# Scale and shift on ScalarE in the opening, two weight operands made there, and LayerNorm, swish, gates and combining issued in separate steps

## The chip, the cores and the metric

The kernel runs on one core of one Trainium2 chip. The metric is the device time of one execution in microseconds (us). Three runs of the kernel before gave 2275.82, 2274.79 and 2270.39 us, with a median of 2274.79.

Five engines work side by side, each with its own queue that it works off in order: TensorE (PE) multiplies matrices, VectorE (DVE) and ScalarE (ACT) do elementwise work and can read PE's results in PSUM, GpSimd (POOL) does elementwise work in SBUF, and SyncE (SP) issues most of the DMAs. An instruction that waits for another engine holds up all that stands behind it in its queue.

## The reference

One layer of a hybrid decoder in float32, for 2048 tokens of a prompt and 8 single tokens (samples), model width 1024:

```python
shift, scale, gate = split(c @ w_c + b_c, 3)
h = x * (1 + scale) + shift
q, k, v, ga, glu, gb, ma, mb = split(h @ w_in + b_in)        # 8704 columns
# A: 12 heads in 3 groups (window, dilation) = (128,1), (512,4), (2048,16), causal, with ALiBi;
#    head j of the three groups is combined, weighted by the groups' softmax denominators
a = (o * silu(ga)) @ w_pa
# B: u = glu; causal depthwise convolution of width 31 -> LayerNorm over 512 channels -> swish
b = (conv * silu(gb)) @ w_pb
y = (sigmoid(ma) * a + sigmoid(mb) * b) @ w_o
x_out = LayerNorm(alpha * x + gate * y)
```

Further outputs are the last k and v rows of each group and the convolution's state.

## The kernel before, in words

**Products.** `h @ w_in` is made in two halves of 1024 tokens (`p` = 0 and 1). Each half is again two blocks of 512 tokens, and the columns of w_in come in pairs of 128-wide tiles. One such pair, over two token blocks and two halves of the inner dimension, is done by a Strassen-like scheme with seven products instead of eight (`quad`, L551). Its left operands (OPS, L34) are sums and differences of the blocks of h, its right operands b11, b21, b22, T1 to T4 are tiles of w_in and differences of them. Every operand is split into a high part, rounded to fp32r by ACT, and a low part, the rest, made by DVE or POOL (L238, L247), and each product is three matmuls: high by high, low by high and high by low (`product`, L489). In the first half a column pair takes 14 products 258 wide (256 tokens and two samples each), in the second half 7 products 512 wide. Products go to PSUM banks X, Z, Y and W; ACT copies part of them out (c1, u2, u3), DVE adds those to the others with the bias and writes a staged tile zst.

**Weights.** `w_make` (L235) makes one right operand: ACT's copy, then the subtraction. `on_dve` (2) gives two of seven of these subtractions to DVE, the others to POOL. In the first half `w_make` also forms T1 to T4 on DVE and stores them to memory; the second half loads them. `MAKE` (L501) and `ahead` (L527) say after which product which operand is made; the second half makes them four products ahead.

**Opening** (L283 to L421). In four blocks b of 256 input columns: 32 matmuls on w_c (`mod_block`), transposes of x into banks X, Y, Z, W (`prep_first`), a copy of the modulation (mrow) and its transposes to scale and shift (`mod_finish`, modT), then `prep_mod`: `part` scales and shifts a transposed block into f (DVE), copies the samples' few columns (ACT), and the seven left operands are formed and split on ACT, DVE and POOL. x is loaded in blocks of 1024 rows by 256, in two buffers. After the opening, operands b11, b21, T2 and T1 of the first pair are made, and the products begin.

**The order of the rest** is set by a count of time kept while the program is written out (`clock`, in us, raised by the estimated length of every product). After every product (in the second half also in the middle of one) `tick` (L474) is called. It takes a step of each lane whose time has come. A lane is a generator, and its `yield 2.6` asks for its next step 2.6 later on that count: `rows_lane` (rows of k and v, and small ends), `at_lane` (attention), `mix_lane` (in the first half samples, then `conv_norm`; in the second `conv_norm`, `combine`, `early_out`) and `smp_lane` (attention of the samples). Convolution steps on DVE fill the rest. `later` puts off a DMA by 2.6.

The parts of it that the change touches:

- `ev_gate` (L705): t = z + bias; ACT's tanh of it into h_; DVE's (h_ + 1) * t, the gate, and its store. All are issued at once.
- `stats` (L817): DVE's mean and variance, three small POOL instructions for rstd and the offset (`rstd_of`, L761), and ACT's Identity that normalizes from PSUM, issued at once.
- `swish` (L828): two ACT instructions and DVE's multiplication, issued at once.
- `conv_norm` (L847): pieces of 256 tokens: load, transpose, `stats` twice, transpose back, `swish` four times, times the gate, store.
- `attention` (L1145): its output Uo has one buffer, which is written by DVE and POOL and stored by DMA.
- `combine` (L1321): 32 items, each a load of three groups' rows; `factors_a` (DVE, then ACT's exponential), `factors_b` (DVE, then ACT scales the first group), `weigh` (four DVE multiply-adds), `turn` (PE transposes, DVE multiplies by the gate, store). One iteration, three steps 1.3 apart: load x and weigh x - 2; factors_a of x - 1; factors_b of x - 1 and turn x - 2.
- `early_out` (L1425) follows `combine` in its lane: it loads and splits w_pa.

A last stage (from L1567) makes a, b, y and the final LayerNorm. It begins with `oc_load`, the loads of what combining and `conv_norm` have stored.

Of the kernel before, what the change touches and what calls it, by code (L numbers as in the profile page):

```python
# [11 lines left out]
OP = mybir.AluOpType  # L12
# [34 lines left out]
def hybrid_layer(ctx: ExitStack, tc: tile.TileContext, I, O):  # L47
# [149 lines left out]
    def w_raw(s, e, x):  # L197
        p, n = stream[s]
        col = col_of(quads[p][n][x])
        if p == 0 and s and e and x:  # L200
            r = raws[s, e, x] = bp.tile([P, 4, P], F32, name="rawb", tag="rawb", bufs=2)
# [33 lines left out]
    def w_make(s, n):  # L235
# [22 lines left out]
        if n == "b11":  # L258
            split(R(0, 0))
        elif n == "b21":  # L260
            split(R(1, 0))
            sub(R(0, 0), R(0, 1), R(0, 0), "T1")
        elif n == "T2":
            t2 = bp.tile([P, 4, P], F32, name="t2", tag="t2")
            sub(t2, R(1, 1), R(0, 0), "T2")
            split(t2)
            sub(R(1, 0), R(1, 0), t2, "T4")
        elif n == "T1":
            split(R(0, 0))
            sub(R(0, 1), R(1, 1), R(0, 1), "T3")  # L270
        elif n == "T3":
            split(R(0, 1))
        elif n == "b22":
            split(R(1, 1))
        else:
            split(R(1, 0))
            for k in [k for k in raws if k[0] == s]:
                raws.pop(k)
# [13 lines left out]

    def x_load(b):
        xs[b] = st.tile([P, 8, 256], F32, name="xs", tag="xs", bufs=2)
        ld(xs[b], I["x_prompt"][0, 0:1024, b * 256:(b + 1) * 256].rearrange("(t p) n -> p t n", p=P))

# [60 lines left out]
    def prep_first(b):  # L357

        pxs = []
        for t in range(2):  # L360
            for e in range(2):
                px = ps("XYZW"[2 * t + e])
                for i in range(4):
                    PE.transpose(px[:, i * P:(i + 1) * P], xs[b][:, 4 * t + i, e * P:(e + 1) * P], ident)
                pxs.append(px)
        pq = ps("U", (P, 2, NB))
        for e in range(2):
            PE.transpose(pq[:, e, :], xsm[:, (2 * b + e) * P:(2 * b + e + 1) * P], ident[:NB, :NB])
        return pxs, pq

    def prep_mod(b, pxs, pq):
# [4 lines left out]
        def part(t, e):  # L376
            kt = 2 * b + e
            f = F[t, e] = st.tile([P, 2 * SUB], F32, name=f"f{t}{e}", tag=f"f{t}{e}")
            v = subs_view(f)
            DVE.tensor_scalar(v[:, :, 0:256], pxs[2 * t + e].rearrange("p (s n) -> p s n", s=2), s1T[:, kt, 0:1], shT[:, kt, 0:1],  # L380
                              op0=OP.mult, op1=OP.add)
            ACT.activation(v[:, :, 256:258], hs[:, e, 4 * t:4 * t + 4].rearrange("p (s n) -> p s n", s=2), AF.Copy)
            return f
# [6 lines left out]
        f["a11"] = part(0, 0)  # L390
        split("a11", DVE)
        f["a12"] = part(0, 1)
        split("a12", POOL)
        part(1, 0)
        f["a22"] = part(1, 1)
        xs.pop(b)
        if b + 2 < 4:
            x_load(b + 2)
        DVE.tensor_tensor(f["s1"], F[1, 0], F[1, 1], op=OP.add)
# [9 lines left out]
    biases()  # L409
    cur = None  # L410
    for b in range(4):
        pm = mod_block(b)
        pre = prep_first(b)
        if b == 0:
            x_load(1)
        if b == 1:
            w_load(0, 0)
            w_load(0, 1)
        mod_finish(b, pm)
        prep_mod(b, *pre)  # L420
    closed(st_cm)  # L421
    bp_cm, bp = opened("bp0", bufs=1)
    wp_cm, wp = opened("wp0", bufs=1)
# [77 lines left out]
    MAKE = {8: (1, "b11"), 9: (1, "b21"), 11: (1, "T2"), 13: (1, "T1"), 0: (0, "T3"), 3: (0, "b22"), 5: (0, "T4")}  # L501
    made = set()

# [201 lines left out]
    def ev_gate(dst, kept, j, col):  # L705
# [3 lines left out]
        def ev(a, u, c, sub):  # L709
            n0, n, sm = span(c, sub)  # L710
            t = stage()
            h_ = stage()
            th = h_[:, :n]
            m = n if sm is None else n + 2
            out_of(t[:, :m], a[:, :m], None if u is None else u[:, :m], b)
            samples_of(kept[:, j, sm], t, sm, n)
            ACT.activation(th, t[:, :n], AF.Tanh, scale=0.5)
            vstt(t[:, :n], th, 1.0, t[:, :n], OP.add, OP.mult)
            gone(h_)
            store(dst[:, c * 512 + n0:c * 512 + n0 + n], t, n)  # L720
        return ev
# [95 lines left out]
    def stats(cv, px, m, out):  # L817
# [7 lines left out]
        POOL.tensor_scalar(sm[:m, 3:4], sm[:m, 0:1], sm[:m, 2:3], -1.0, op0=OP.mult, op1=OP.mult)  # L825
        ACT.activation(out, px[:m], AF.Identity, bias=sm[:m, 3:4], scale=sm[:m, 2:3])

    def swish(pt, yv, i):  # L828
        ACT.activation(yv, pt, AF.Tanh, bias=cgb[:, i, 1:2], scale=cgb[:, i, 0:1])
        ACT.activation(pt, pt, AF.Identity, bias=cgb4[:, i, 1:2], scale=cgb4[:, i, 0:1])  # L830
        vstt(yv, yv, 1.0, pt, OP.add, OP.mult)

    def norm_samples(cv):
        nrm = cv.tile([P, 1054], F32, name="y", tag="y", bufs=2)[:NB, 0:512]
        px = ps("S")
        for i in range(4):
            PE.transpose(px[:NB, i * P:(i + 1) * P], ysS[:, i, :], ident)
        stats(cv, px, NB, nrm)
        yield 6.0
        pt = ps("S", (P, 4, NB))  # L840
        for i in range(4):
            PE.transpose(pt[:, i, :], nrm[:, i * P:(i + 1) * P], ident[:NB, :NB])
        for i in range(4):
            swish(pt[:, i, :], ysS[:, i, :], i)
        yield 1.0

    def conv_norm(cv):  # L847
# [10 lines left out]
        load(pieces[0])  # L858
        yield 5.0
        for x in pieces:  # L860
# [4 lines left out]
            for k in range(2):  # L865
# [3 lines left out]
                clock["pe"] += 0.44  # L869
                stats(cv, px, P, nrm[:, k, :])  # L870
                yield 2.0
            if x + 1 in pieces:
                load(x + 1)
            yield 4.0
            for h in range(2):
# [5 lines left out]
                for i in range(2):  # L881
                    yv = y[:, 2 * h + i, :]
                    swish(pt[:, i, :], yv, 2 * h + i)
                    vtt(yv, yv, sg[:, 2 * h + i, :], OP.mult)
                yield 4.0
            later(lambda y=y, x=x: ld(cg_d[:, :, 256 * x:256 * x + 256].rearrange("i p n -> p i n"), y))
# [258 lines left out]
    def attention(ra, g, j, p, tab, gap, loads, last):  # L1145
# [72 lines left out]
        def s_pv(i):  # L1218
# [4 lines left out]
            for n, (b, prev, s) in enumerate(segs(bts[i])):  # L1223
# [4 lines left out]
                clock["pe"] += 0.22 if prev else 0.11  # L1228
            Uo = ra.tile([P, 4, 130], F32, name="Uo", tag="Uo")
            vcopy(Uo[:, :nb, :P], U[:, :nb, :])  # L1230
# [90 lines left out]
    def combine(cv):  # L1321
# [52 lines left out]
        n = len(work)  # L1374
        for x in range(n + 2):

# [114 lines left out]
    queued = set()  # L1491
    for n in ("b11", "b21", "T2", "T1"):
        make(0, n)
    s = 0
    for p in range(2):
# [44 lines left out]
        if p == 0:  # L1540
# [262 lines left out]
```

## Time and profile before

| what | value |
|---|---|
| median of 3 runs | 2274.79 us |
| the profiled execution | 2272.58 us |
| its span, first to last instruction | 2270.7 us |
| granted TensorE clock, mean over the span | 0.981 |
| instructions | 36385 |
| moved by DMA | 392.08 MB, 173 GB/s |

The page of the profile lists each engine's busy time, the span in 40 slices, the DMA queues, the chain of work that ended last, and the costliest groups of instructions with what ended the idle time before them. Views of the trace show the same by line, by wait, by stretch of time (windows) or in order of time. In a timeline's row stand the start in us, the duration, the engine, the line, the operation, the tiles (written<-read) and the shapes; square brackets hold the idle time of the engine just before it and what ended that. In a row of waits stand the us in total, the number of times and the longest. A line can be that of a helper: L76 and L80 are the helpers for DVE's two-input operations.

### The profile page before, as it was taken

How to read it: one execution, taken by the hardware profiler on the slowest of the kernel's cores; microseconds unless marked ns; L12 is line 12 of the kernel's file. 1: busy time of each engine (PE TensorE's matmuls, PEld its weight loads, DVE VectorE, ACT ScalarE, POOL GpSimd, SP SyncE). 2: the span in 40 equal slices, each digit the busy share in tenths (PEclk: the TensorE clock that was granted, in tenths of full speed). 3: DMA queues.
4: the chain of work that ended last, by engine and by line, in shares of the span. 5: the costliest groups of instructions: out<-in, count | busy, mean ns of one | idle time of the engine just before them, and what ended most of it. 6: DMA issues, size and time to landing. Idle time of an engine off the chain costs nothing.

```text
span 2270.7 us, 36385 instructions
## 1 busy us (share of the span) xinstructions
PE 2124.6 (94%) x13185; PEld 1866.6 (82%) x13185; DVE 1375.4 (61%) x2205; ACT 909.4 (40%) x2056; POOL 833.6 (37%) x866
## 2 busy tenths in 40 slices
PE   6799999999997899989999999999988888999998
PEld 3699999999997768968888888888776667888886
DVE  4667776777676633445777777644556635554556
ACT  2424444444444435644444443456454442111110
POOL 1445454444543333453333333333212235322332
PEclk9899999999999999999999999999999999999999
DMA  8255554456667665445555555568878657334220
GB/s 254 87 171 185 151 180 147 152 163 193 200 201 248 189 195 178 153 111 156 161 178 166 176 148 179 185 191 261 252 237 235 214 176 252 113 121 130 94 95 30
DMA packets 403981, 392.08 MB, mean 173 GB/s; under 512 B 26521, under 2 KB 331213, under 8 KB 402769
## 3 DMA queue, kind: packets, MB, share of 16 engines
q1 hardware_dynamic: 336213, 342.63, 48.8%
q10 hardware_dynamic: 67588, 47.13, 6.5%
q8 instruction: 104, 1.70, 0.3%
q14 instruction: 76, 0.62, 0.1%
HBM read 245.91 MB, written 144.29 MB: 172 GB/s over the span
## 4 chain that ended last, share of the span: by engine, by line
PE 46%; DVE 6%; issue 5%; ACT 4%; DMA 3%; POOL 3%; ACTq 0%; SPq 0%; POOLq 0%; DVEq 0%
PE ps_W L494 8%; PE ps_X L494 8%; PE ps_Z L494 8%; PE py L1743 7%; PE pab L1687 5%; PE ps_Y L494 4%; PE ps_S L1187 3%; PE ps_U L979 1%; POOL bop L247 1%; PE ps_U L1227 1%; DVE yL L76 1%; ACT bop L238 1%; PE ps_S L1212 1%; DVE zst L80 1%; DMA orow<-Uo 1%
## 5 line engine op out<-in xcount | busy, mean ns | idle before, releaser
L247 POOL TENSOR_TENSOR bop<-raw,bop 128x512 fp32r<-128x512 f32 x273 | 397.9, 1459 | 643.2 <-ACT bop L238 584.6
L494 PE MATMUL ps_W<-As,bop 128*128 128x258 f32 (+1 forms) x2448 | 438.8, 328 | 20.5 <-DVE zst L80 19.4
L494 PEld LDWEIGHTS ps_W<-As,bop 128*128 128x128 f32 x2448 | 361.5, 191 | 62.8 <-DVE zst L80 23.6
L80 DVE SCALAR_TENSOR_TENSOR y<-u,cwT,y 128x1024 f32<-128x1024 f32 x240 | 361.1, 1505 | 1.6
L238 ACT ACTIVATE bop<-raw 128x512 fp32r<-128x512 f32 x409 | 251.5, 624 | 79.6 <-DVE raw L76 27.7
L494 PE MATMUL ps_X<-Aa,bop 128*128 128x258 f32 (+1 forms) x1224 | 220.9, 329 | 22.3 <-ACT bop L238 14.0
L494 PE MATMUL ps_Z<-As,bop 128*128 128x258 f32 (+1 forms) x1224 | 224.5, 330 | 7.0 <-ACT u L575 5.7
L494 PE MATMUL ps_X<-As,bop 128*128 128x258 f32 (+1 forms) x1224 | 220.5, 326 | 2.8 <-POOL As L1112 2.2
L494 PE MATMUL ps_Y<-Aa,bop 128*128 128x258 f32 (+1 forms) x1224 | 221.3, 329 | 0.0
L494 PEld LDWEIGHTS ps_X<-Aa,bop 128*128 128x128 f32 x1224 | 183.2, 194 | 43.7 <-ACT bop L238 14.3
L494 PE MATMUL ps_Z<-Aa,bop 128*128 128x258 f32 (+1 forms) x1224 | 217.1, 326 | 1.3 <-ACT smg L605 1.3
L247 DVE TENSOR_TENSOR bop<-raw,bop 128x512 fp32r<-128x512 f32 x136 | 100.6, 739 | 182.1 <-ACT bop L238 178.2
L494 PEld LDWEIGHTS ps_Z<-As,bop 128*128 128x128 f32 x1224 | 180.9, 192 | 27.3 <-ACT u L575 6.3
L494 PEld LDWEIGHTS ps_X<-As,bop 128*128 128x128 f32 x1224 | 179.6, 191 | 22.1 <-POOL As L1112 3.0
L494 PEld LDWEIGHTS ps_Z<-Aa,bop 128*128 128x128 f32 x1224 | 181.0, 191 | 20.1 <-ACT smg L605 1.5
L494 PEld LDWEIGHTS ps_Y<-Aa,bop 128*128 128x128 f32 x1224 | 181.9, 193 | 18.2 <-issue 1.8
L1204 ACT ACTIVATE X<-X,mz 128x128 f32<-128x128 f32 (+1 forms) x192 | 87.0, 454 | 167.8 <-DVE mz L84 160.5
L80 DVE SCALAR_TENSOR_TENSOR zst<-ps_W,bT,c 128x258 f32<-128x258 f32 (+1 forms) x102 | 58.4, 573 | 92.7 <-ACT c L585 90.6
L1640 ACT ACTIVATE xr<-xr,lnm 128x1024 f32<-128x1024 f32 (+1 forms) x16 | 19.9, 1244 | 183.8 <-POOL lnm L1639 183.8
L1687 PE MATMUL pab<-oH,wc0H 128*128 128x256 f32 (+1 forms) x256 | 73.5, 287 | 18.5 <-DVE ev L80 16.1
L1187 PE MATMUL ps_S<-ak,aq 128*128 128x256 f32 (+1 forms) x256 | 90.3, 484 | 0.0
L80 DVE SCALAR_TENSOR_TENSOR zst<-ps_Y,bT,c 128x258 f32<-128x258 f32 (+1 forms) x90 | 51.4, 571 | 56.2 <-PE ps_Y L494 36.5
(309 smaller groups left out, 3743.0 us busy)
## 6 DMA issues: line engine op xcount, KB each, us to landing
raw<-w_in SPq DMA_DIRECT2D x205, 256.0 KB
raw<-tw_d SPq DMA_DIRECT2D x136, 256.0 KB
tw_d<-raw SPq DMA_DIRECT2D x102, 256.0 KB
tw_d<-t SPq DMA_DIRECT2D x34, 256.0 KB
rawb<-w_in SPq DMA_DIRECT2D x33, 256.0 KB
wc<-w_c SPq DMA_DIRECT2D x16, 512.0 KB
aq<-zq SPq DMA_DIRECT2D x16, 512.0 KB
xr<-x_prompt SPq DMA_DIRECT2D x16, 512.0 KB
```

Source lines behind the costliest of these rows:

```text
L76: DVE.tensor_tensor(out, a, b, op=op)
L80: DVE.scalar_tensor_tensor(out, a, s, b, op0=op0, op1=op1)
L238: ACT.activation(t[:, 0], r, AF.Copy)
L247: eng.tensor_tensor(t[:, 1], r, f32(t[:, 0]), op=OP.subtract)
L494: PE.matmul(acc[:, :n], w[:, i, b, :], a[:, b, off:off + n], start=start and b == 0 and x == 0, stop=b == 3 and x == 2, skip_group_check=True)
L979: PE.matmul(po, PZ[:n, g, x, :], t[:n, g, :], start=x == 0 and g == 0, stop=x == NB - 1 and g == 2)
L1187: PE.matmul(S[:, s:s + w, :], q_of(b), k_of(b, w), start=True, stop=True)
L1204: ACT.activation(X[:, s:s + w, :], X[:, s:s + w, :], AF.Exp, bias=mz[:, n, 0:1], accum_out=mz[:, n, 1:2])
L1212: PE.transpose(pt[:, s, :], X[:, s, :], ident)
L1227: PE.matmul(U[:, n, :], Y[:, s, :], v_of(b), start=not prev, stop=True)
L1687: PE.matmul(p[:, :n], a, b[:, kt, :n], start=i == 0, stop=i == 11)
L1743: PE.matmul(py[h], a[:, d, c0:c0 + P], w[:, h * 512:(h + 1) * 512], start=f, stop=l)
```

## The change

- **Opening.** `part`'s scale and shift is an ACT Identity with scale and bias instead of a DVE tensor_scalar, and the samples' columns are copied by POOL instead of ACT. The order of the four parts is a11, a21, a22, a12. x is loaded in half blocks of 512 rows, with three buffers, each half issued when a buffer is free. Operands b11 and b21 of the first pair are made in block 3, ahead of its `mod_finish`; for that, their pool is opened before the opening, and two tiles (rawb, t2) move to another pool.
- **Gates, LayerNorm, swish.** The gate's last multiplication and store are a step of rows_lane 1.4 later. `stats` returns its normalizing activation, and `conv_norm` issues it 2.6 later. The swish's multiplication is issued 2.6 after its activations. The first load of `conv_norm` has 9.0 instead of 5.0 ahead of its use.
- **Combining.** One iteration is now: load x and factors_b of x - 2; factors_a of x - 1; turn x - 3 and weigh x - 2. There is one iteration more.
- **Attention.** Uo has two buffers.
- **Second half.** `on_dve` is 0: all subtractions of the right operands are POOL's.

```diff
+    def x_load(b, ts=(0, 1)):
+        for t in ts:
+            xs[b, t] = st.tile([P, 4, 256], F32, name="xs", tag="xs", bufs=3)
...
-            DVE.tensor_scalar(v[:, :, 0:256], pxs[2 * t + e].rearrange("p (s n) -> p s n", s=2), s1T[:, kt, 0:1], shT[:, kt, 0:1],
-                              op0=OP.mult, op1=OP.add)
-            ACT.activation(v[:, :, 256:258], hs[:, e, 4 * t:4 * t + 4].rearrange("p (s n) -> p s n", s=2), AF.Copy)
+            ACT.activation(v[:, :, 0:256], pxs[2 * t + e].rearrange("p (s n) -> p s n", s=2), AF.Identity, scale=s1T[:, kt, 0:1],
+                           bias=shT[:, kt, 0:1])
+            POOL.tensor_copy(v[:, :, 256:258], hs[:, e, 4 * t:4 * t + 4].rearrange("p (s n) -> p s n", s=2))
...
-        xs.pop(b)
+        if b + 1 < 4:
+            x_load(b + 1, (1,))
         if b + 2 < 4:
-            x_load(b + 2)
+            x_load(b + 2, (0,))
...
+        if b == 3:
+            w_make(0, "b11")
+            w_make(0, "b21")
         mod_finish(b, pm)
         prep_mod(b, *pre)
...
-            vstt(t[:, :n], th, 1.0, t[:, :n], OP.add, OP.mult)
-            gone(h_)
-            store(dst[:, c * 512 + n0:c * 512 + n0 + n], t, n)
+            def end(at):
+                while clock["pe"] < at:
+                    yield 0.3
+                vstt(t[:, :n], th, 1.0, t[:, :n], OP.add, OP.mult)
+                gone(h_)
+                store(dst[:, c * 512 + n0:c * 512 + n0 + n], t, n)
+            rows_lane.add(end(clock["pe"] + 1.4))
...
-        ACT.activation(out, px[:m], AF.Identity, bias=sm[:m, 3:4], scale=sm[:m, 2:3])
+        return lambda: ACT.activation(out, px[:m], AF.Identity, bias=sm[:m, 3:4], scale=sm[:m, 2:3])
...
-                stats(cv, px, P, nrm[:, k, :])
-                yield 2.0
+                apply = stats(cv, px, P, nrm[:, k, :])
+                yield 2.6
+                apply()
...
+                yield 2.6
+                for i in range(2):
+                    yv = y[:, 2 * h + i, :]
+                    swish_end(pt[:, i, :], yv)
                     vtt(yv, yv, sg[:, 2 * h + i, :], OP.mult)
-                yield 4.0
+                yield 1.3
...
-            Uo = ra.tile([P, 4, 130], F32, name="Uo", tag="Uo")
+            Uo = ra.tile([P, 4, 130], F32, name="Uo", tag="Uo", bufs=2)
...
-        for x in range(n + 2):
+        for x in range(n + 3):
...
             if 0 <= x - 2 < n:
-                weigh(x - 2)
+                factors_b(x - 2)
             yield 1.3
             if 0 <= x - 1 < n:
                 factors_a(x - 1)
             yield 1.3
-            if 0 <= x - 1 < n:
-                factors_b(x - 1)
+            if 0 <= x - 3 < n:
+                turn(x - 3)
             if 0 <= x - 2 < n:
-                turn(x - 2)
+                weigh(x - 2)
             yield 1.3
...
+            on_dve[0] = 0
```

More of the change, by code (lines that the diff above doesn't have):

```diff
@@ L200, in w_raw @@
         if p == 0 and s and e and x:
-            r = raws[s, e, x] = bp.tile([P, 4, P], F32, name="rawb", tag="rawb", bufs=2)
+            r = raws[s, e, x] = wp.tile([P, 4, P], F32, name="rawb", tag="rawb", bufs=2)
         else:
@@ L263, in w_make @@
         elif n == "T2":
-            t2 = bp.tile([P, 4, P], F32, name="t2", tag="t2")
+            t2 = wp.tile([P, 4, P], F32, name="t2", tag="t2")
             sub(t2, R(1, 1), R(0, 0), "T2")
@@ L291, in wc_load @@
         ld(wcs[b, h, k], I["w_c"][k * 512:(k + 1) * 512, h * D + b * 256:h * D + (b + 1) * 256].rearrange("(k p) n -> p k n", p=P))
-    def x_load(b):
-        xs[b] = st.tile([P, 8, 256], F32, name="xs", tag="xs", bufs=2)
-        ld(xs[b], I["x_prompt"][0, 0:1024, b * 256:(b + 1) * 256].rearrange("(t p) n -> p t n", p=P))
+    def x_load(b, ts=(0, 1)):
+        for t in ts:
+            xs[b, t] = st.tile([P, 4, 256], F32, name="xs", tag="xs", bufs=3)
+            ld(xs[b, t], I["x_prompt"][0, 512 * t:512 * t + 512, b * 256:(b + 1) * 256].rearrange("(t p) n -> p t n", p=P))
     HK = ((0, 0), (0, 1), (1, 0), (1, 1))
@@ L363, in prep_first @@
                 for i in range(4):
-                    PE.transpose(px[:, i * P:(i + 1) * P], xs[b][:, 4 * t + i, e * P:(e + 1) * P], ident)
+                    PE.transpose(px[:, i * P:(i + 1) * P], xs[b, t][:, i, e * P:(e + 1) * P], ident)
                 pxs.append(px)
@@ L391, in prep_mod @@
         split("a11", DVE)
+        part(1, 0)
+        f["a22"] = part(1, 1)
         f["a12"] = part(0, 1)
         split("a12", POOL)
-        part(1, 0)
-        f["a22"] = part(1, 1)
-        xs.pop(b)
+        if b + 1 < 4:
+            x_load(b + 1, (1,))
         if b + 2 < 4:
-            x_load(b + 2)
+            x_load(b + 2, (0,))
         DVE.tensor_tensor(f["s1"], F[1, 0], F[1, 1], op=OP.add)
@@ L409, in hybrid_layer @@
     biases()
-    cur = None
+    bp_cm, bp = opened("bp0", bufs=1)
     for b in range(4):
@@ L414, in hybrid_layer @@
         if b == 0:
-            x_load(1)
+            x_load(1, (0,))
         if b == 1:
@@ L421, in hybrid_layer @@
     closed(st_cm)
-    bp_cm, bp = opened("bp0", bufs=1)
     wp_cm, wp = opened("wp0", bufs=1)
@@ L501, in hybrid_layer @@
     MAKE = {8: (1, "b11"), 9: (1, "b21"), 11: (1, "T2"), 13: (1, "T1"), 0: (0, "T3"), 3: (0, "b22"), 5: (0, "T4")}
-    made = set()
+    made = {(0, "b11"), (0, "b21")}
     def make(s, n):
@@ L830, in swish, with swish_end @@
         ACT.activation(pt, pt, AF.Identity, bias=cgb4[:, i, 1:2], scale=cgb4[:, i, 0:1])
+    def swish_end(pt, yv):
         vstt(yv, yv, 1.0, pt, OP.add, OP.mult)
@@ L837, in norm_samples @@
             PE.transpose(px[:NB, i * P:(i + 1) * P], ysS[:, i, :], ident)
-        stats(cv, px, NB, nrm)
-        yield 6.0
+        apply = stats(cv, px, NB, nrm)
+        yield 4.0
+        apply()
+        yield 4.0
         pt = ps("S", (P, 4, NB))
@@ L844, in norm_samples @@
             swish(pt[:, i, :], ysS[:, i, :], i)
+        yield 2.0
+        for i in range(4):
+            swish_end(pt[:, i, :], ysS[:, i, :])
         yield 1.0
@@ L858, in conv_norm @@
         load(pieces[0])
-        yield 5.0
+        yield 9.0
         for x in pieces:
@@ L869, in conv_norm @@
                 clock["pe"] += 0.44
-                stats(cv, px, P, nrm[:, k, :])
-                yield 2.0
+                apply = stats(cv, px, P, nrm[:, k, :])
+                yield 2.6
+                apply()
             if x + 1 in pieces:
                 load(x + 1)
-            yield 4.0
+            yield 2.6
             for h in range(2):
@@ L883, in conv_norm @@
                     swish(pt[:, i, :], yv, 2 * h + i)
+                yield 2.6
+                for i in range(2):
+                    yv = y[:, 2 * h + i, :]
+                    swish_end(pt[:, i, :], yv)
                     vtt(yv, yv, sg[:, 2 * h + i, :], OP.mult)
-                yield 4.0
+                yield 1.3
             later(lambda y=y, x=x: ld(cg_d[:, :, 256 * x:256 * x + 256].rearrange("i p n -> p i n"), y))
@@ L1491, in hybrid_layer @@
     queued = set()
-    for n in ("b11", "b21", "T2", "T1"):
+    for n in ("T2", "T1"):
         make(0, n)
```

## The prediction

> **What bounds the kernel now.** I read the page's busy table first, then the view of windows, stage by stage, and then the engines' own timelines where TensorE (PE) stands still.
>
> ```profile
> span 2270.7 us, 36385 instructions
> PE 2124.6 (94%) x13185; PEld 1866.6 (82%) x13185; DVE 1375.4 (61%) x2205; ACT 909.4 (40%) x2056; POOL 833.6 (37%) x866
> ```
>
> PE is busy for 94% of the span, so at most 2270.7 - 2124.6 = 146 us of standing still can be won, beside what a lowered clock costs; the matmuls themselves stay as they are. The windows say where those 146 us lie. Their columns: stretch, its length, then busy us (instructions) of PE, PEld, DVE, ACT and POOL, the granted clock, the DMA share and GB/s.
>
> ```profile
> 0.00:84.00 84.00, 48.20 (x239) 25.42 (x240) 49.39 (x74) 21.04 (x47) 18.39 (x18) 0.85 0.57 172
> 84.00:655.00 571.00, 567.36 (x4581) 559.12 (x4581) 393.70 (x550) 248.72 (x614) 279.13 (x321) 1.00 0.55 170
> 655.00:820.00 165.00, 134.46 (x993) 127.67 (x992) 104.24 (x202) 76.22 (x175) 58.96 (x108) 0.94 0.71 216
> 955.00:1012.00 57.00, 46.10 (x216) 36.67 (x215) 29.85 (x33) 30.83 (x62) 35.27 (x29) 0.94 0.32 94
> 1012.00:1520.00 508.00, 507.35 (x2420) 418.02 (x2419) 342.42 (x374) 221.39 (x485) 168.27 (x146) 1.00 0.56 169
> 1610.00:1725.00 115.00, 101.94 (x485) 83.79 (x483) 68.37 (x199) 55.17 (x162) 22.78 (x26) 0.96 0.80 245
> 1725.00:1826.00 101.00, 86.04 (x364) 65.17 (x365) 69.20 (x209) 46.18 (x107) 25.11 (x20) 0.98 0.71 222
> ```
>
> The long stretches of products, 84 to 655 and 1012 to 1520, have 3.6 and 0.7 us of PE idle in them: whatever the change does to evictions, Uo or splits there is hidden. The idle is in the opening (35.8 us), in the stretch with gates, LayerNorm and swish of the first half (30.5), at the turn between the halves (10.9), and in the combining (13.1 + 15.0). The change has a part in each, so I cost it stage by stage. In each the question is which instruction, waiting at the head of an in-order queue, holds back the work behind it.
>
> **The opening.** Rows of DVE, ACT, POOL and PE from their timelines; the last two are prices from elsewhere.
>
> ```profile
> 53.71 0.20 DVE L352 TENSOR_TENSOR modT<-ps_S,mbias 128x36 f32<-128x36 f32 x1 [0.50 <-PE ps_S L350]
> 67.95 0.20 DVE L352 TENSOR_TENSOR modT<-ps_S,mbias 128x36 f32<-128x36 f32 x1 [0.50 <-PE ps_S L350]
> 70.66 0.81 DVE L380 TENSOR_SCALAR f<-ps_Y,modT 128x512 f32<-128x512 f32 x1
> 79.74 1.35 DVE L387 TENSOR_TENSOR Aa<-f,Aa 128x516 fp32r<-128x516 f32 x1 [0.43 <-ACT Aa L386]
> 82.24 1.75 DVE L76 TENSOR_TENSOR raw<-raw 128x512 f32<-128x512 f32 x1 [1.15 <-POOL bop L247]
> 84.03 0.69 DVE L76 TENSOR_TENSOR t<-raw 128x512 f32<-128x512 f32 x1
> 84.76 0.63 ACT L238 ACTIVATE bop<-t 128x512 fp32r<-128x512 f32 x1 [4.01 <-DVE t L76]
> 85.47 1.28 POOL L247 TENSOR_TENSOR bop<-t,bop 128x512 fp32r<-128x512 f32 x1 [2.02 <-ACT bop L238]
> 80.28 0.80 PE L494 MATMUL ps_X<-Aa,bop 128*128 128x258 f32 x2 [12.37 <-ACT bop L238]
> 86.34 1.94 PE L494 MATMUL ps_X<-As,bop 128*128 128x258 f32 x12
> 768.82 0.78 ACT L826 ACTIVATE y<-ps_S,lnm 128x512 f32<-128x512 f32 x1 [3.38 <-POOL lnm L825]
> 762.07 0.18 POOL L611 COPY smg<-zst 128x2 f32<-128x2 f32 x1 [6.06 <-DVE zst L80]
> ```
>
> A block of the opening lasts 67.95 - 53.71 = 14.2 us, and DVE is its chain: the next block's mrow copy stands behind all of this block's DVE work. The change takes four scale-and-shifts of 0.81 (3.2 us) off DVE and gives them to ACT, where this operation on this shape does not occur; the nearest row is the LayerNorm's Identity from PSUM at 0.78, so about the same, on an engine that is idle most of the block. The small copies go to POOL at 0.18 each. DVE now waits for ACT before its first sum, so I let 2.0 of the 3.2 come through (bounds 0 and 3.2). That holds for two blocks. Ahead of block 3's mrow the change puts a subtraction that waits for POOL (1.75 for itself, and some 0.6 of waiting), so that block gains nothing: 2.0 - 2.4 = -0.4. The last modT comes 3.6 us earlier.
>
> Now the end. Today PE stands 12.37 us for operand b11, because its ACT copy is behind all of block 3. With b11 and b21 made beforehand the first two products run as soon as a11 and a12 are there. The third product needs T2, which still stands behind block 3 on DVE: today DVE ends block 3 at 79.74 + 1.35, 13.1 after modT, and with the 2.0 off at 11.1; then come 0.69, 0.63 and 1.28 (subtraction, ACT, POOL). It starts some 12.4 us after modT, and its third matmul waits until 13.7. Today it starts 86.34 - 67.95 = 18.4 after. I count from the later one, 18.4 - 13.7 = 4.7 won, not 12.37: T2 is late next. Opening: 3.6 + 4.7 = **-8** (bounds -4, if DVE keeps its pace, and -12.4, all of today's wait). The x loads go in halves, with three buffers of half the size; the second half of block 2 is now issued behind the w_in loads on SP, and PE's matmuls on w_c for that block hide its landing; were it late, PE's transposes and DVE's next block would be late by as much.
>
> **Gates, LayerNorm, swish (first half).** A row of the list of ACT's waits, then PE's timeline, and one row of DVE.
>
> ```profile
> ACT y L826 <- POOL lnm L825: 46.8, 16, 6.8
> 697.24 1.09 PE L868 MATMUL ps_S<-ident,u 128*128 128x128 f32 x4 [5.80 <-DMA u<-ysp_d]
> 770.17 2.00 PE L494 MATMUL ps_X<-Aa,bop 128*128 128x258 f32 x12 [2.97 <-ACT smg L605]
> 801.93 2.82 PE L494 MATMUL ps_Z<-As,bop 128*128 128x258 f32 x12 [4.60 <-ACT u L575]
> 667.30 1.60 PE L494 MATMUL ps_Y<-Aa,bop 128*128 128x258 f32 x12
> 658.28 0.43 DVE L80 SCALAR_TENSOR_TENSOR zst<-zst 128x256 f32<-128x256 f32 x1 [0.48 <-ACT zst L717]
> ```
>
> The normalizing activation is issued as soon as its statistics are, and ACT stands 46.8 / 16 = 2.9 us in the mean until POOL has the rstd. Behind it in ACT's queue are the copies that empty PE's banks: that is PE's 2.97 and 4.60. Issued 2.6 later (two ticks, two products of about 1.5), it finds its operand ready, or waits under 1 us. DVE's finishing multiply waits 0.48 for each gate's tanh, and the swish's the same way; behind these are the evictions of bank W. Moved behind other work, both go. The load of u had 5.0 and now has 9.0 to land, so of its 5.80 some 1.5 stay. New waits: PSUM tile S is held longer, and POOL's rstd can stand behind a split. Of 30.5 us I leave 10: **-20** (bounds -10 and -27). Standing still also slows the matmuls after it: 2.82 instead of 1.60. At a granted clock of 0.94 that is 6% of 134.46 = 8 us, of which I take **-5** back (bounds 0 and -8). The same steps in the second half meet no idle and bring nothing.
>
> The Trainium skill ("TensorE: Matmul & The Clock Gate", section on HAM oscillation) has it that the clock drops only behind idle gaps of over about 3.4 us. By that, only three of these gaps (5.80, 4.60 and one in the combining) count and the clock terms would shrink to about half, the sum to some 2230; the trace is less strict, with 2.00 for 1.60 behind a gap of 2.97.
>
> **Splits to POOL, and the turn.** From page part 5, and PE's timeline:
>
> ```profile
> L247 POOL TENSOR_TENSOR bop<-raw,bop 128x512 fp32r<-128x512 f32 x273 | 397.9, 1459 | 643.2 <-ACT bop L238 584.6
> L247 DVE TENSOR_TENSOR bop<-raw,bop 128x512 fp32r<-128x512 f32 x136 | 100.6, 739 | 182.1 <-ACT bop L238 178.2
> 990.59 0.73 PE L494 MATMUL ps_X<-As,bop 128*128 128x512 f32 x2 [1.70 <-POOL As L1112]
> ```
>
> Two in seven splits are DVE's, so 68 of the second half's 238 move to POOL: DVE sheds 68 x 0.74 = 50 us and the waits ahead of them (178.2 / 136 = 1.3 each), POOL gains 68 x 1.46 = 99. One product of the second half is 507 us in 2420 matmuls, 2.5 us a dozen, so POOL keeps up. Only at the turn, where PE already waits for POOL's As, does it bite: one or two splits in the way, **+2** (0 to +4).
>
> **Combining.** PE, then DVE and POOL beside it, then the earlier worst case, then DVE's waits within 1725 to 1826.
>
> ```profile
> 1764.95 0.69 PE L1365 MATMUL ps_S<-ident,y 128*128 128x128 f32 x2 [3.04 <-issue]
> 1762.11 3.01 DVE L80 SCALAR_TENSOR_TENSOR y<-y,csf 128x128 f32<-128x128 f32 x4 [1.04 <-ACT y L1351]
> 1756.17 1.18 DVE L80 SCALAR_TENSOR_TENSOR u<-u,csf 128x128 f32<-128x128 f32 x4
> 1761.86 1.26 POOL L247 TENSOR_TENSOR bop<-raw,bop 128x512 fp32r<-128x512 f32 x1 [3.37 <-ACT bop L238]
> 1674.93 0.74 PE L1365 MATMUL ps_S<-ident,u 128*128 128x128 f32 x2 [5.76 <-DVE u L80]
> 1673.40 0.69 DVE L88 COPY Uo<-ps_U 128x512 f32<-128x512 f32 x1 [6.80 <-DMA orow<-Uo]
> DVE bop L247 <- ACT bop L238: 13.8, 8, 2.1
> DVE csf L76 <- ACT csf L1341: 8.3, 13, 1.6
> ```
>
> PE's transposes stand until DVE has weighed their rows. Weigh and turn were two ticks apart and become three (some 1.5 us more); DVE's waits of 13.8 and 8.3 go, with the splits moved and the exponentials a tick older; the second Uo buffer takes the 6.80. DVE's 69.2 + 27 of waits in 101 us becomes about 80, below PE's 86. Of 28.1 us I leave 9: **-19** (bounds -9 and -25), and of the clock's 6 us (0.04 x 102 + 0.02 x 86) I take **-4**. Loads now wait on SP for the turn four items back, with the fetches of weights queued behind them, five operands ahead of use; a store of that turn's result waited there a tick later already, so I cost it at nothing.
>
> **Handing over.** Combining runs one item more, about 5 us, and the early output weights and the last stage's loads follow it. From the chain and PE's timeline:
>
> ```profile
> 1855.45 6.59 DMA ocr<-cg_d
> 1864.27 0.39 PE L1687 MATMUL pab<-oH,wc0H 128*128 128x256 f32 x1 [2.29 <-ACT oH L1587]
> ```
>
> That load already arrives last, so its delay is PE's: **+5** (0 to +6).
>
> **Sum.** -8 - 20 - 5 + 2 - 19 - 4 + 5 = -49. The profiled execution took 2272.58 us (1.9 beyond its span) and becomes 2223.6; the median of 2274.79 lies 2.2 higher, so 2226. A measurement of this kernel tells about 0.3% (7 us) from no change.
>
> **Rivals.** (1) *The waits move on instead of going.* POOL's rstd comes 2.9 us late today and is asked for 3 us later; behind a longer POOL queue ACT waits anew, and DVE, near PE's pace in combining, keeps turns late. Half of every gain: -4 - 10 - 2.5 - 9.5 - 2 + 7 = -21, so 2254. For it: four stages, all with thin margins. Against: the worst single waits (12.37, 5.80, 5.76, 4.60) each have a clear remedy here.
>
> (2) *POOL's extra splits block DVE.* Beside two POOL splits DVE's four multiplies took 3.01 instead of 1.18, 0.9 for each split. 68 more put up to 68 x 1.46 = 99 us in DVE's way; if each reached PE through a late eviction, the time is 2226 + 99 = 2325, slower than before. It decides from 49 / 68 = 0.72 us of PE time a split. Against it: DVE is busy 342 of 508 us from 1012 to 1520, and 342 + 99 - 50 fits with 117 to spare.
> The Trainium skill ("SBUF — State Buffer", section "Who interferes with whom") says that a VectorE instruction with two SBUF inputs and a GpSimd one that reads SBUF share a port pair, and the later one blocks entirely; by that rule alone this rival stands, and the 3.01 beside 1.18 agrees.
>
> (3) *No net change*: the handover takes more, or memory now shared between opening and products makes b11 wait after all, and the other stages bring little: 0 - 5 + 4 - 9 + 6 = -4, so 2271.
>
> **Chances.** Forecast 0.70, (1) 0.20, (2) 0.05, (3) 0.05. The range reaches down to the sum with all gains near their bounds (4, 7, 6 and for the clock 4 us more: 2205), and up to rival (1), 2254. Faster by over 0.3%: 0.70 + 0.20 = 0.90; within: 0.05; slower: 0.05.
>
> **What would show it.** First product of the opening near 66, third near 78; no ACT wait for lnm above 1 us and PE idle of about 10 us in the gates' stretch; turn's waits under 10 us together; the start of the last stage waiting 5 us longer for ocr. I am wrong if the long product stretches show PE idle for evictions or bop, or if the clock stays at 0.94 to 0.96 without gaps.

## The result, and the profile after

The new kernel takes 2204.66 us, the median of four runs (2202.19 to 2208.26), against 2272.59 (2268.56 to 2275.82) for the kernel before: a ratio of 0.9703, with a 95% interval of 0.968 to 0.9726. That is 68 us less, where 49 were forecast; the median lies at the very edge of the range, 0.3 us below it. The profiled execution took 2208.26 us, and its span is 64.3 us shorter than the one before. The head of the new page:

```profile
span 2206.4 us, 36413 instructions
PE 2109.8 (96%) x13185; PEld 1864.7 (85%) x13185; DVE 1333.1 (60%) x2121; ACT 918.3 (42%) x2056; POOL 930.2 (42%) x950
```

PE is busy for 14.8 us less with the same number of matmuls, and stands still for 97 us instead of 146: so about 50 us are waits that are gone, and 15 us are matmuls that run faster or overlap better. Where that lies is read from windows cut at nearly the same work in both traces (opening, gates' stretch, combining; the counts of matmuls differ by 4 at most). Before, then after; the columns are those of the prediction:

```profile
0.00:86.30 86.30, 50.50 (x253) 27.72 (x254) 51.13 (x77) 22.47 (x50) 19.23 (x19) 0.84 0.57 173
644.00:820.00 176.00, 145.46 (x1084) 138.48 (x1084) 110.73 (x216) 81.78 (x188) 64.62 (x116) 0.94 0.68 210
1607.00:1857.00 250.00, 220.50 (x982) 174.88 (x981) 148.15 (x420) 118.09 (x295) 61.89 (x54) 0.97 0.73 229
```

```profile
0.00:78.50 78.50, 48.85 (x254) 28.02 (x254) 39.47 (x61) 31.61 (x50) 22.92 (x35) 0.89 0.62 191
634.00:787.00 153.00, 135.45 (x1080) 130.75 (x1078) 112.92 (x210) 78.82 (x181) 66.78 (x104) 0.99 0.77 239
1578.80:1794.00 215.20, 210.08 (x985) 173.14 (x983) 145.26 (x404) 115.62 (x294) 85.09 (x72) 0.98 0.85 265
```

The gates' stretch is 23 us shorter: idle 30.5 becomes 17.5, and PE's busy time falls by 10.0 for nearly the same matmuls, with the granted clock at 0.99 instead of 0.94. (By the finer measure below the whole first half wins 20.2, so the stretch won 20 to 23.) Combining is 34.8 us shorter: idle 29.5 becomes 5.1, busy falls by 10.4.

For the experiments a finer measure is wanted. Every run has the same products in the same order, so the start of one product in the trace of before, less its start in another trace, is what that run has won up to there. The marks are the third product of the opening, the first product 512 wide (the start of the second half), the second half's products 100, 165 (ahead of combining) and 237 (its end); the differences between them belong to the stages. In us, with the positive sign for earlier:

| kernel | opening | first half | turn | to product 165 | combining | span |
|---|---|---|---|---|---|---|
| new | 7.9 | 20.2 | -4.0 | 3.3 | 36.1 | 64.3 |
| new, profiled again (e9) | 7.8 | 20.2 | -3.6 | 3.3 | 39.0 | 66.7 |
| e1: opening alone | 7.9 | -1.2 | -0.1 | 0.1 | 1.7 | 7.9 |
| e2: combining's old order | 7.0 | 19.6 | -1.5 | 3.3 | 16.5 | 45.1 |
| e3: splits on DVE too | 8.0 | 19.7 | 0.1 | 2.9 | 25.6 | 55.6 |
| e4: one Uo buffer | 7.1 | 15.7 | -3.6 | 3.3 | 32.7 | 55.4 |
| e5: norm at once | 8.1 | 11.2 | -1.9 | 1.1 | 40.6 | 57.4 |
| e6: gates at once | 7.4 | 23.8 | -3.6 | 2.1 | 37.5 | 66.5 |
| e7: load 5.0 ahead | 7.0 | 14.4 | -1.8 | 2.7 | 37.6 | 59.4 |
| e8: three iterations more | 6.3 | 20.8 | -1.9 | 3.1 | 36.6 | 50.1 |
| e10: T2 in block 3 | 11.9 | 19.2 | -3.8 | 3.3 | 36.6 | 66.8 |
| e11: switch after the turn | 7.1 | 21.3 | 1.5 | 3.3 | 38.4 | 70.0 |
| e12: e10 and e11 | 11.8 | 21.3 | 1.6 | 3.3 | 38.8 | 76.6 |

The eight runs whose code of combining is the new one won between 36.1 and 40.6 us there, two runs of one kernel 36.1 and 39.0. So one trace places a gain in combining to within some 4 us. At the turn, nine runs with the new kernel's code there fall into two groups: -3.6 to -4.0 in five, -1.5 to -1.9 in four (e2, e5, e7, e8). So a figure of one trace can be off by over 2 us there.

Now the places. In the opening, PE and then DVE and ACT of the new kernel:

```profile
64.50 0.59 PE L351 MATMUL ps_S<-ident,mrow 9*128 9x9 f32 x4 [5.71 <-DVE mrow L348]
66.18 2.95 PE L498 MATMUL ps_X<-Aa,bop 128*128 128x258 f32 x12 [1.10 <-ACT f L381]
78.47 3.07 PE L498 MATMUL ps_X<-As,bop 128*128 128x258 f32 x12 [6.67 <-ACT c L568]
```

```profile
65.12 0.19 DVE L353 TENSOR_TENSOR modT<-ps_S,mbias 128x36 f32<-128x36 f32 x1 [0.68 <-PE ps_S L351]
76.28 0.68 DVE L76 TENSOR_TENSOR t<-raw 128x512 f32<-128x512 f32 x1
```

```profile
77.00 0.63 ACT L238 ACTIVATE bop<-t 128x512 fp32r<-128x512 f32 x1 [2.01 <-DVE t L76]
77.53 0.61 ACT L238 ACTIVATE bop<-raw 128x512 fp32r<-128x512 f32 x1
78.05 0.37 ACT L568 ACTIVATE c<-ps_X 128x258 f32<-128x258 f32 x1
```

The first product starts at 66.18 (forecast: near 66), the third at 78.47 (near 78). The third waits 6.67 us, and what ends the wait is not T2 itself: the product writes bank X, and the copy that empties X stands on ACT behind T2's copy, which waits for DVE's t. The head of a queue holds back what is behind it, here once more.

At the turn, PE and POOL:

```profile
963.56 1.22 PE L498 MATMUL ps_X<-As,bop 128*128 128x512 f32 x2 [3.38 <-POOL As L1133]
964.58 5.11 PE L498 MATMUL ps_Z<-Aa,bop 128*128 128x512 f32 x12
```

```profile
958.42 3.42 POOL L247 TENSOR_TENSOR bop<-raw,bop 128x512 fp32r<-128x512 f32 x2
961.80 1.71 POOL L1133 TENSOR_TENSOR As<-Fs,As 128x512 fp32r<-128x512 f32 x1
```

Two splits stand ahead of As in POOL's queue, as forecast; the wait of 1.70 became 3.38, and the product behind it takes 5.11 us instead of 2.95 (the kernel before at 991.16).

For combining, PE's waits from 1530 to 1830, before and after:

```profile
PE ps_S L1365 <- issue: 10.7, 6, 3.0
PE ps_S L1365 <- DVE u L80: 9.0, 4, 5.8
```

```profile
PE ps_S L1386 <- issue: 2.2, 1, 2.2
```

and those of DVE from 1570 to 1830 before. After, DVE makes no split here, and the same waits are 1.5 us for csf and 2.6 for Uo:

```profile
DVE bop L247 <- ACT bop L238: 31.4, 16, 3.4
DVE csf L76 <- ACT csf L1341: 16.4, 22, 1.6
DVE Uo L88 <- DMA orow<-Uo: 16.0, 5, 6.8
```

### The profile page after: what moved, and what is told of

Its sections match the earlier page's. It is cut to its first block, busy times and chain, and to the rows that moved or that the text cites. A ratio compares the mean times of both kernels' runs of the same rounds, so it can differ in the third digit from the quotient of the medians.

```text
span 2206.4 us, 36413 instructions
## 1 busy us (share of the span) xinstructions
PE 2109.8 (96%) x13185; PEld 1864.7 (85%) x13185; DVE 1333.1 (60%) x2121; ACT 918.3 (42%) x2056; POOL 930.2 (42%) x950
## 4 chain that ended last, share of the span: by engine, by line
PE 53%; DVE 4%; DMA 2%; issue 1%; POOL 1%; ACT 1%; ACTq 0%; SPq 0%; POOLq 0%; DVEq 0%
PE ps_Z L498 9%; PE ps_W L498 9%; PE ps_X L498 9%; PE py L1765 8%; PE pab L1709 5%; PE ps_Y L498 4%; PE ps_S L1208 3%; PE ps_U L1248 1%; PE ps_S L1233 1%; DVE yL L76 1%; PE ps_S L653 1%; DVE xr L80 1%; PE ps_U L1246 1%; DVE st L1648 0%; DMA u<-orow 0%
## 5 line engine op out<-in xcount | busy, mean ns | idle before, releaser
L247 POOL TENSOR_TENSOR bop<-raw,bop 128x512 fp32r<-128x512 f32 x341 | 485.8, 1430 | 568.2 <-ACT bop L238 441.3
L247 DVE TENSOR_TENSOR bop<-raw,bop 128x512 fp32r<-128x512 f32 x68 | 51.9, 763 | 94.4 <-ACT bop L238 90.9
L80 DVE SCALAR_TENSOR_TENSOR X<-ps_S,tabh 128x512 f32<-128x512 f32 (+1 forms) x80 | 52.5, 656 | 83.0 <-PE ps_S L1208 76.0
L1662 ACT ACTIVATE xr<-xr,lnm 128x1024 f32<-128x1024 f32 (+1 forms) x16 | 19.9, 1244 | 183.7 <-POOL lnm L1661 171.2
```

The costliest lines, as they stand in the source:

```text
L80: DVE.scalar_tensor_tensor(out, a, s, b, op0=op0, op1=op1)
L247: eng.tensor_tensor(t[:, 1], r, f32(t[:, 0]), op=OP.subtract)
```

## The experiments

The theory: PE stood still because an instruction that waited at the head of an in-order queue (DVE's for a split, an exponential or a store; ACT's for rstd) held back the eviction or the weighing that PE needed; the change removes those waits one by one, each worth its own part. The main rivals: the waits move on and share one gain; POOL's splits block DVE; the handover's step.

**The opening alone (e1).** The kernel before with the opening's part of the diff only.

> The kernel before with the opening's part of the change alone (and the splits moved to POOL in the second half and the new order in combining both left as the new kernel has them is NOT the case here: gates, LayerNorm, swish, Uo are as before; combining and on_dve are as in the new kernel). Theory (each stage keeps what its own waits lose): products of the long stretch start 7 us earlier, the gates' stretch keeps its 30 us of idle, combining gains 20 to 35 us: 2205 + 21 to 25 for the gates' stretch and 3 to 7 for Uo, so 2229 to 2237. Rival (the waits move on, the stages share one gain): removing the gates' steps costs under 10 us, 2205 to 2215.

This text describes another kernel, one with the new combining in it, and its numbers are not for the one that ran, so nothing was forecast for it. By the stages of the traces the opening alone gives its own 8 us, 2265, but that is worked out after the fact. Measured: 2264.92 us, ratio 0.9971 (0.996 to 0.9982), 8.2 us under the 2273.09 of before. The 7.9 us that stand in the table at the third product are still there at the end. So the gain in the opening isn't eaten by later stages.

**Combining's old order (e2).**

```diff
-        for x in range(n + 3):
+        for x in range(n + 2):
...
-                factors_b(x - 2)
+                weigh(x - 2)
...
-            if 0 <= x - 3 < n:
-                turn(x - 3)
+            if 0 <= x - 1 < n:
+                factors_b(x - 1)
             if 0 <= x - 2 < n:
-                weigh(x - 2)
+                turn(x - 2)
```

> The new kernel with combining's old order (weigh x-2; factors_a of x-1; factors_b of x-1 and turn of x-2), all else new. Theory (the order takes the waits for ACT's exponential and for weigh off the heads of the queues): combining loses 15 to 30 of the 35.5 us that it won, 2220 to 2235, with DVE waiting 8 us or more for csf and PE waiting 15 us or more at the turn's transposes. Rival (splits moved to POOL and the second Uo buffer did it by themselves): within 6 us of the new kernel.

2228.06 us, ratio 0.9809 (0.9795 to 0.9822): 23 us over the new kernel. PE's and DVE's waits in combining:

```profile
PE ps_S L1386 <- issue: 10.2, 6, 3.0
PE ps_S L1386 <- DVE u L80: 4.1, 1, 4.1
```

```profile
DVE csf L76 <- ACT csf L1362: 25.9, 25, 2.3
```

The waits at the turn's transposes and those for the exponential are back together. The order is worth some 21 us of combining (16.5 against 36 to 41). How much of that is the later turn and how much the older exponential was not separated.

**Two of seven splits on DVE (e3)**: the line `on_dve[0] = 0` is left out.

> The new kernel with two of seven splits on DVE in the second half, as before. Theory (splits at the head of DVE's queue wait for ACT's copy): the turn gets back 3 us, combining loses 5 to 15, so slower than the new kernel by 2 to 12 us, 2207 to 2217. Rival of the prediction (POOL's extra splits block DVE): faster than the new kernel by 5 us or more. Second rival (with the new order nothing in combining waits for DVE): 2202, faster by the turn's 3 alone.

2216.64 us, ratio 0.9761 (0.9748 to 0.9774): 12 us over the new kernel, the upper end of what the theory gave. The table has 4 us given back at the turn and 10 to 13 lost in combining, where DVE waits again:

```profile
DVE bop L247 <- ACT bop L238: 31.7, 16, 4.3
```

The rival of the prediction had the sign the other way: moving these splits to POOL is worth 12 us net, and the turn is the only place where this trace shows a cost of it.

**One Uo buffer (e4)**: without `bufs=2`.

> The new kernel with one Uo buffer. Theory (a copy into Uo that waits for the store holds DVE's queue): DVE's waits on that store come back, 7 to 13 us in combining, of which PE sees 3 to 7: 2208 to 2212. Rival (hidden behind the deeper order of combining): within 2 us of the new kernel.

2216.36 us, ratio 0.9756 (0.9743 to 0.9769): 12 us over the new kernel, more than either theory gave. DVE's waits on the store are back in combining (20.6 us from 1570 to 1830, where 7 to 13 were expected), and combining loses 3 to 6 us. Another 4.5 are lost in the first half's products, 3.6 of them at one place, which I had counted as covered. PE there, a window around it, and the same place in the kernel before, PE and DVE:

```profile
370.05 2.95 PE L498 MATMUL ps_W<-As,bop 128*128 128x258 f32 x12 [2.08 <-DVE zst L80]
372.80 1.92 PE L498 MATMUL ps_Z<-As,bop 128*128 128x258 f32 x12
```

```profile
369.00:374.00 5.00, 3.95 (x20) 3.95 (x21) 3.55 (x6) 0.35 (x1) 3.00 (x4) 0.66 0.24 79
```

```profile
375.70 1.70 PE L494 MATMUL ps_W<-As,bop 128*128 128x258 f32 x12 [1.98 <-DVE zst L80]
373.63 0.42 DVE L88 COPY Uo<-ps_U 128x256 f32<-128x256 f32 x1 [4.36 <-DMA orow<-Uo]
```

On DVE of e4, a copy into Uo starts 2.1 us ahead of that product, after 4.46 us of idle time, with the eviction of W behind it in the queue. Its row names a product as what ended the wait; the row of the kernel before, for the same copy, names the store of the tile before. In e4 the wait of 2.08 us is followed by products at a granted clock of 0.66 that take 2.95 and 1.92 us instead of 1.60. In the kernel before, a wait of 1.98 us was followed by one of 1.70. So of these 3.6 us the change won about 2 here, the wait; the slow products are e4's own (the last section says what decides on them).

**The norm's activation at once (e5)**: `stats` issues it and returns an empty function.

> The new kernel with LayerNorm's normalizing activation issued at once behind its statistics, as before; all else new. Theory (at the head of ACT's queue it waits 3 us for POOL's rstd, and the copies that empty PE's banks stand behind it): ACT waits 35 to 47 us for lnm again, and of the 21 us that the gates' stretch won, 8 to 15 go: 2213 to 2220. Rival (the waits had moved on to POOL, so the late step brings little): within 4 us of the new kernel.

The samples' small norm uses `stats` too; the change gave it the same later step, and this edit takes it back with the other. 2216.89 us, ratio 0.9753 (0.9735 to 0.9771): 12 us over the new kernel. ACT waits 39.3 us for the offset again, 15.2 of them between 630 and 830, and PE there for copies that stand behind it:

```profile
ACT y L835 <- POOL lnm L834: 15.2, 7, 3.1
```

```profile
PE ps_X L498 <- ACT u L579: 6.6, 3, 3.5
PE ps_Z L498 <- ACT zst L609: 3.0, 1, 3.0
```

The first half loses 9 us, and the second half's norm, where the prediction had seen nothing to win, another 2.

**The gate's end at once (e6).**

```diff
-            rows_lane.add(end(clock["pe"] + 1.4))
+            for _ in end(clock["pe"]):
+                pass
```

> The new kernel with the gate's last multiplication and store issued at once, as before. Theory (DVE waits 0.5 us for each of the gates' tanh at the head of its queue, with evictions behind it): 2 to 6 us slower, 2207 to 2211. Rival (DVE has time for these short waits, and the gain of the stretch is LayerNorm's and the load's): within 2 us.

2204.13 us, ratio 0.9697 (0.9679 to 0.9715): no different from the new kernel. Its trace is 3.6 us better in the first half, but that isn't in the median. The later step for the gates brings nothing that can be measured.

**The first load 5.0 ahead (e7)**: `yield 5.0` for `yield 9.0`.

> The new kernel with 5.0 instead of 9.0 between the first load of the convolution's rows and their transposes. Theory (the load takes longer than 5 us, and PE stands for what is left): the first transpose of the first half waits 3 to 6 us again, 2207 to 2211 in all. Rival (the later steps of the norm give the load its time anyhow): within 2 us.

2212.27 us, ratio 0.9732 (0.9714 to 0.9749): 8 us over the new kernel. The wait is back, and with it the slower clock, 0.94 from 634 to 787 where the new kernel has 0.99:

```profile
PE ps_S L884 <- DMA u<-ysp_d: 4.6, 1, 4.6
```

**Combining ends three iterations later (e8)**: `range(n + 6)`.

> The new kernel with three more empty iterations behind combining (six more than items, not three), so that what follows in its lane, the early output weights, comes three iterations later. The prediction's step (the handover is on the path: an iteration more costs its 5 us): about 15 us slower, 2218 to 2222, with PE waiting longer ahead of the last stage's first matmul. Rival (the last turn ends some 34 us ahead of the last stage, so there is slack): within 3 us of the new kernel.

2221.23 us, ratio 0.9772 (0.9753 to 0.9791): 17 us over the new kernel. The prediction's step holds, for these iterations. PE, ACT and SP of this run at the start of the last stage:

```profile
1811.61 0.58 PE L1709 MATMUL pab<-oH,wc0H 128*128 128x256 f32 x1 [14.59 <-ACT oH L1609]
```

```profile
1798.15 2.95 ACT L1439 ACTIVATE wc0H<-xr 128x1024 fp32r<-128x1024 f32 x3 [0.40 <-ACT zst L698]
1810.51 1.06 ACT L1609 ACTIVATE oH<-ocr 128x1024 fp32r<-128x1024 f32 x1 [9.40 <-DMA ocr<-og_d]
```

```profile
1800.49 3.61 SPq L53 DMA_DIRECT2D xr<-w_pb x3
1804.20 0.39 SPq L53 DMA_DIRECT2D ocr<-og_d  x1
```

Three of the four early weights are split only behind the last product; SP's loads of w_pb wait for their buffers, and the loads of ocr stand behind them. In the new kernel the same chain, followed back from the end, reads:

```profile
1789.01 2.89 DVE wc0L L1440
1792.78 7.75 DMA ocr<-cg_d
```

That load lands at 1800.53, and ACT has just come to it: its copy oH starts at 1799.62, bH at 1800.61. In the kernel before it landed at 1862.04 (1855.45 + 6.59), and ACT came to bH only at 1864.13. So there were 2.1 us of slack, and the one iteration that the change adds used them up. PE's wait there in the new kernel:

```profile
1800.73 0.38 PE L1709 MATMUL pab<-oH,wc0H 128*128 128x256 f32 x1 [2.29 <-ACT oH L1609]
```

It is as long as before. Three iterations more make it 14.59 - 2.29 = 12.3 us longer, 4.1 for each. The last stage behind that wait takes another 3.3 us more than in the new kernel, and its clock is lower at the start (0.69 from 1811.6 to 1823, where the new kernel has 0.85 from 1800.7 to 1812).

**T2 inside block 3 (e10), the switch of the splits after the turn (e11), both (e12)**, with the new kernel run again beside them (e9). e10 leaves only the split of b21 ahead of mrow and makes T1's difference and T2 behind the block's four scale-and-shifts; e11 sets `on_dve` in the second half's second quad:

```diff
+        if b == 3:
+            w_make(0, "T2")
         if b + 1 < 4:
             x_load(b + 1, (1,))
```

```diff
-            on_dve[0] = 0
...
-            at_tick[s + 1, 5] = lambda: (sample_gates(), leave("fp"))
+            at_tick[s + 1, 5] = lambda: (sample_gates(), leave("fp"), on_dve.__setitem__(0, 0))
```

> The new kernel once more, unchanged, beside the three variants that follow, as their base: 2202 to 2208.

> The new kernel with T1's subtraction moved behind the last mrow copy, and T2 (subtraction, ACT's copy, POOL's rest) made inside block 3, behind its four scale-and-shifts; T4's subtraction follows later. Theory (the two waits left in the opening, 5.71 us for mrow and 6.67 us for T2, are DVE's order alone): mrow comes 2 to 3 us earlier, the wait for T2 falls under 3 us, and the whole is 4 to 8 us faster: 2197 to 2201. Rival (DVE's chain of block 3 is the bound, so what is put into it comes out behind it): the left operands come later by as much as T2 comes earlier, within 2 us of the new kernel.

> The new kernel with the switch to POOL for all splits put twelve products later (on_dve set to 0 in the second half's second quad instead of ahead of its first). Theory (at the turn two right operands' splits lie ahead of POOL's As, so PE's wait of 3.38 us is theirs): that wait falls under 1.5 us and the whole is 2 to 4 us faster, combining as in the new kernel. Rival (PE waits at the turn for evictions and operands of the same chain on ACT anyhow): within 1 us.

> Both edits of the two runs before together. Theory: the gains add, 6 to 12 us faster than the new kernel, 2193 to 2199. Rival (one of them is hidden): the larger alone.

| kernel | median us | ratio to before | 95% interval |
|---|---|---|---|
| e9, the new kernel again | 2206.17 | 0.9706 | 0.9693 to 0.9719 |
| e10 | 2205.51 | 0.97 | 0.9687 to 0.9714 |
| e11 | 2204.19 | 0.9698 | 0.9684 to 0.9711 |
| e12 | 2195.92 | 0.9669 | 0.9656 to 0.9683 |

PE in e10's opening, and in e11's turn:

```profile
61.27 0.46 PE L358 MATMUL ps_S<-ident,mrow 9*128 9x9 f32 x4 [2.82 <-DVE mrow L355]
74.40 2.95 PE L507 MATMUL ps_X<-As,bop 128*128 128x258 f32 x12 [5.39 <-ACT c L577]
```

```profile
960.79 0.72 PE L498 MATMUL ps_X<-As,bop 128*128 128x512 f32 x2 [1.70 <-POOL As L1133]
961.35 2.95 PE L498 MATMUL ps_Z<-Aa,bop 128*128 128x512 f32 x12
```

In e10 the third product comes 4.1 us earlier, 3.2 of it from mrow. The wait ahead of it is still 5.39 us where under 3 was expected, since the copy out of bank X now stands behind block 3's own splits on ACT. In e11 the turn is 5.1 us better than in e9, and the product behind the shorter wait takes 2.95 again; but 1.4 of the 5.1 lie ahead of that wait, and e5, e7 and e8 have the same 1.4 without the edit. Each alone moves the median by less than its trace shows (0.7 and 2.0 us against e9, within the intervals), and combining in both traces gains no more than in e9. Both together are 10.3 us faster than e9. That is at least the sum of what the two traces show at their places (4.1 and 3.7, or 5.1 with the 1.4). Why the single edits don't show their parts in the median stays open. e12 is the fastest kernel of this study.

## Why the prediction was right and where not

**Direction and mechanism: right.** The change was to work by taking waits off the heads of queues, stage by stage, and e1 to e5 and e7 show parts that add up: opening 8; order of combining 21, splits 12 and Uo 3 to 6 make the 36 to 39 of combining; norm 9, load 6 and Uo 4.5 make the 20 of the first half (with Uo at 2, as in the trace of before, 17). Rival 1, half of every gain, falls. Rival 2 falls by e3. Rival 3's shared memory showed no wait.

**Opening, -8: right** (7.9), with both times as forecast, in part by two errors that cancel: the last modT came 2.8 us earlier instead of 3.6, the third product 13.35 us behind it, so 5.0 won there instead of 4.7. What PE waits for is the copy of bank X behind T2's copy.

**Gates, norm and swish, -20 and -5 for the clock: the sum right, the split wrong.** The window gives 23 us: 13 of idle, since 17.5 are left where I left 10, and 10 of busy time, all of the clock's 8 and some overlap. ACT's waits for the norm's offset fell from 46.8 us in 16 to 7.2 in 5; the longest is 3.1, where I wanted none above 1. The 46.8 were of the whole trace: 27.0 of them lay between 630 and 830, the rest in the second half. The gates' part of the story, DVE's 0.48 for each tanh, was worth nothing (e6).

**The turn, +2: too small** (+4.0). The wait is the forecast one; the 2.2 us of slow product behind it were not in my count. In e5, e7 and e8 the turn loses only 1.8 to 1.9, as the clock is back earlier there, ahead of this wait.

**The second half's norm, nothing: wrong by 3.** "Meet no idle" is nearly true: the idle that went between the products 130 and 165 is 1.4 us. The other 2 us are the same matmuls in less time, and e5, which keeps only 1.1 of the 3.3, says that they come with the norm's late step.

**Combining, -19 and -4, and the handover, +5: this is the step that was mis-sized**, -18 for what measured -36. Three terms erred one way. Idle: I left 9 us "of 28.1", 5.1 stayed of 29.5, since the three causes (exponential, splits, Uo) went together. Busy time: -4 for the clock, -10.4 measured. The clock itself accounts for about 5: its slow stretches in this window, at half speed, add up to 17.1 us before and 6.8 after. They stand behind the longer of the turn's waits, as behind the last one before:

```profile
1824.70 0.55 PE L1365 MATMUL ps_S<-ident,y 128*128 128x128 f32 x2 [2.15 <-issue]
1825.00 4.55 PE L494 MATMUL ps_Z<-Aa,bop 128*128 128x512 f32 x12
```

That product takes 2.95 elsewhere. The other 5 us are the same matmuls closer together at full clock, which the sum had no term for; what makes them was not tested. Handover: "that load already arrives last, so its delay is PE's" overlooked the slack: the load landed 2.1 us ahead of its reader, and the first product of the last stage waited for ACT's copy of the other load, behind the last tanh. Past that slack the sentence is true (e8), but the delay was not 5. The first early weight is loaded 5.4 us later against the last tanh (30.5 us ahead of it, before 35.9), and the last ACT copy of the four starts 19.9 us after that load instead of 25.4, so the load of ocr was issued 6.2 us ahead of that tanh instead of 7.0. I had priced the extra iteration and not followed the four splits behind it. Why they now come closer together was not tested.

**The signs.** First and third product came as stated, and the turn's waits fell under 10 us together (2.5). Two failed: an ACT wait for the offset above 1 us is left, with 17.5 us of idle in the gates' stretch, and the last stage doesn't wait longer for ocr.

**What was not tried**: to bring the copy out of bank X, or the loads of ocr, forward in their queues; both stand as what is late next.

## What to carry to other kernels

When PE stands still, look for the instruction at the head of the in-order queue behind which the needed one stands, and give its operand a step more of time; such a wait pays for itself in a stage where PE is otherwise the bound, if it reaches PE (the gates' did not, e6). Price a wait as itself plus the slow matmuls that may follow it, 1.7 us for each slow slot of the clock in these traces (next section), and for waits of about 2 to 3 us take both cases, with and without. When a stage is made one step longer, follow the loads that come behind it to the end and count the slack: here one step was free, and the next three cost 4.1 us of waiting each and 17 us of the median together.

## What the runs showed of the hardware

Some waits cost more than themselves, and their length alone doesn't say which. PE at the one long wait of combining, in the new kernel and in the same kernel profiled again (e9), and a wait in e5:

```profile
1603.17 0.55 PE L1386 MATMUL ps_S<-ident,y 128*128 128x128 f32 x2 [2.24 <-issue]
1603.47 4.59 PE L498 MATMUL ps_W<-As,bop 128*128 128x512 f32 x12
```

```profile
1602.83 0.55 PE L1386 MATMUL ps_S<-ident,y 128*128 128x128 f32 x2 [2.23 <-issue]
1603.13 3.02 PE L498 MATMUL ps_W<-As,bop 128*128 128x512 f32 x12
```

```profile
738.61 1.72 PE L498 MATMUL ps_Z<-Aa,bop 128*128 128x258 f32 x12 [3.03 <-ACT zst L609]
```

The windows behind the first two, new kernel and e9:

```profile
1604.20:1607.60 3.40, 3.40 (x9) 2.65 (x9) 2.88 (x11) 1.89 (x5) 0.36 (x1) 0.50 1.11 364
```

```profile
1604.40:1607.80 3.40, 3.40 (x17) 3.13 (x16) 2.96 (x13) 2.06 (x5) 0.18 (x1) 1.00 1.10 367
```

Behind 2.24 us the granted clock is 0.50 for 3.4 us, and a product takes 4.59 us instead of 2.95. Behind 2.23 us in the same kernel it stays at 1.00 and the product takes 3.02; behind 3.03 us in e5 it takes 1.72, hardly over its 1.60. The records of the granted clock in the fourteen traces show a pattern. Within each trace the slow stretches start on one grid with slots of 3.41 us and last one slot or several; only the last one ends with the trace. Counted over all traces between 95 and 1790 us, a slot at full clock in which no matmul ran for 55% of the time or more (1.9 us) was followed by a slow one in 83 of 84 cases, one with less than 40% in 3 of 2113, one between in 14 of 60. In the new kernel all of the 2.24 us lie in one slot (1600.8 to 1604.2); in e9 a slot's edge at 1601.1 divides them, and no more than 1.7 of the 2.23 lie in one slot (51%). So with waits of 2 to 3 us the slow clock can differ between two executions of one kernel. A slow slot in which PE is busy throughout costs half its length, 1.7 us. The Trainium skill ("TensorE: Matmul & The Clock Gate", section on HAM oscillation) puts the drop at gaps of over about 3.4 us; the rows here decide, and they show the slow clock behind shorter ones.

The other page that the prediction weighed, the Trainium skill's "SBUF — State Buffer" (section "Who interferes with whom"), would have POOL's splits block DVE. No cost of it reached PE in the long products: with 68 more splits on POOL, 1000 to 1500 has 0.3 us of PE idle in the new kernel's trace, and e3, which puts them back on DVE, is slower.
